# Right sums of layer 1 kept as single products in HBM, and a set order for squares, query copies, weight sums and gated sums

## The chip, the cores and the metric

The kernel runs on one core of one Trainium2 chip. The metric is the device time of one execution in microseconds (us); a kernel is compared by the median of several runs. A core has TensorE (PE, matmuls; PEld are its weight loads), VectorE (DVE), ScalarE (ACT), GpSimd (POOL) and SyncE (SP), each with its own queue of instructions that runs in order. Here SP issues the loads of weights, and POOL issues the small transfers between SBUF and HBM, among them those that add to what stands at their destination. One core needs no exchange with others.

## The reference

A trunk of two layers on 256 tokens of width 2048, in float32. Each layer has an attention part (four differential heads and eight latent heads, one output projection) and a dense MLP of width 8192 with a squared ReLU. Every part is modulated by a conditioning vector. Cut to what matters here:

```python
cond = jax.nn.silu(c)
for l in range(DEPTH):                                   # 2
    mod = cond @ w_ada[l] + b_ada[l]                     # 2048 x 12288
    sh_a, sc_a, g_a, sh_m, sc_m, g_m = split(mod, 6)
    h = _rmsnorm(x) * (1.0 + sc_a) + sh_a
    proj = h @ w_in[l]
    ...                                                  # out_a: differential, out_b: latent attention
    q  = _rmsnorm(cq, q_norm_g[l]) @ w_uq[l]
    kv = _rmsnorm(ckv, kv_norm_g[l]) @ w_ukv[l]
    mix = concatenate([out_a, out_b]) @ w_o[l]           # 2048 x 2048
    x = x + g_a * mix
    h = _rmsnorm(x) * (1.0 + sc_m) + sh_m
    y = square(relu(h @ w_mlp_in[l])) @ w_mlp_out[l]     # 2048 x 8192, 8192 x 2048
    x = x + g_m * y
return _rmsnorm(x, final_norm_g)
```

## The kernel before

**Tiles.** The 256 tokens are two groups t of 128, the 2048 columns of x four groups c of 512; x stays in SBUF. A float32 weight of 1 MB is loaded by SP into a tile `raw` (7 buffers) and split: ScalarE writes its high half `hi` (L158), VectorE the low half `lo` = raw - hi (L161), 4 buffers each. Activations are split likewise, and a product is three matmuls (high by high, low by high, high by low), summed in one of 8 PSUM banks. Intermediate tiles of 256 KB come from a pool of 40 called `u`.

**Order.** Each engine's order comes from the scheduler of the framework, which places instructions as they are written and by its own estimate of when their inputs are there. `behind(a, b)` adds that a stands behind b on their engine without waiting for it.

**Conditioning.** `cond @ w_ada` is done on VectorE: 192 transfers of 1 MB, and for each a multiply that also sums along the row (L387, tile `ada`). `more_ada` puts these sums behind the last `lo` of each weight group, and lets out new transfers at a rate that each stage sets (`RATE_...`): so many per weight group. Each gate or shift is needed at a fixed point later; `ada_need` does what is then still missing.

**w_o.** `rows` makes one column group c of a projection from four weight groups kq (L318, L319: high halves, then L321: low halves, 24 matmuls in each). Behind each c, `updates` lets VectorE multiply the two results by the gate (`yg`, L1425) and add them to x (L1427), and ScalarE square the new x and sum along the row (`sq`, L1441), which the next norm needs.

**Latent queries.** In the attention of layer 1, ScalarE copies query products out of PSUM (`qn`, L353) for the scores (`psm`, L1676), between copies of keys, softmax work and the high halves of `w_uv`.

**The MLP of layer 1** is four blocks fb of 2048 hidden columns. Where `block_by_seven` works, a 2 by 2 block product takes seven products and not eight: `mixed` adds quarters of the activation (`comb`, L1314 to L1317, split into `sh` and `sl`), `seven` adds quarters of the weights (`comb`, L1345 to L1347) and sums seven products over the block in seven banks. The loop over m in steps of 2 makes two columns of hidden tiles and the *left* products (columns 0 to 1023 of the output). At the end of a block `keep` copies each out of PSUM (`part`, L353) and POOL writes or adds it to a tile `kept` in HBM (L1262). The last block (fb = 3) reads the eight left tiles back (`acc`, L1114), combines them (`merged`) and multiplies them by the gate.

`right_by_seven` makes the *right* products (columns 1024 to 2047) of blocks 0 to 2. Its first half takes all eight products directly; its second half takes seven from the mixed halves of the hidden tiles. These were stored in HBM in the loop over m for the last four steps (`stored`, L1172) and are read back (`again`, L1181, tile `sr`), two steps ahead, by POOL. Then `keep_product` adds each of the eight to every output block that it belongs to, by the table `IN_BLOCKS`: 16 entries for four blocks (t, c), so products are added together by the transfers, 15 of them behind the loops. The last block makes its own right columns directly (`last_right`) and adds the four kept blocks to x by `add_rows`: a multiply by the gate on VectorE (L1119), then a transfer that adds to x.

The order around the change is thus set by POOL's single queue (stores, additions, reads in one order), by VectorE's queue, where sums of weights, low halves and combinations share one engine, and by ScalarE's, where high halves, copies and squares do.

Of the kernel before, what the change touches and what calls it, by code (L numbers as in the profile page):

```python
# [19 lines left out]
NK = D // P  # L20
# [49 lines left out]
def consts():  # L70
# [38 lines left out]
class Trunk:  # L109
# [43 lines left out]
    def part(self, raw, i, half, after=None, hi_after=None):  # L153

        v = raw[:, i * half : (i + 1) * half]
        hi = self.wp.tile([P, half], F32R, tag="hi", name=self.name("hi"), bufs=4)
        lo = self.wp.tile([P, half], F32R, tag="lo", name=self.name("lo"), bufs=4)
        ins = self.nc.scalar.activation(hi, v, AF.Copy)  # L158
        if hi_after is not None:
            self.behind(ins, hi_after)  # L160
        ins = self.nc.vector.tensor_tensor(lo, v, hi.bitcast(F32), ALU.subtract)  # L161
        if after is not None:
            self.behind(ins, after)
        return (hi, lo), ins
# [158 lines left out]
    def rows(self, src, xs, c, last=False):  # L323

        pss = [self.bank("pr") for _ in range(2)]
        for kq in range(2 if last else 4):
            if last and kq == 1:
                self.first_squares()
            self.rows_by_k(pss, self.weights(src[c, kq]), xs, kq)
        if last:  # L330
            self.quiet = True
            w = [self.weights(src[c, kq]) for kq in (2, 3)]
            for t in range(2):
                for kq in (2, 3):
                    self.rows_by_k(pss, w[kq - 2], xs, kq, (t,))
        return pss
# [14 lines left out]
    def copy(self, ps, name, scale=1.0):  # L351
        t = self.u(name)
        self.nc.scalar.activation(t, ps, AF.Copy, scale=scale)  # L353
        return t
# [63 lines left out]
    def setup(self):  # L418
        nc, io, cp = self.nc, self.io, self.cp
        self.ada_plan()  # L420
        self.cond = cp.tile([P, D], F32, name="cond")
# [467 lines left out]
    def layer(self, l, acc=None):  # L889
# [31 lines left out]
        q = []  # L921
# [21 lines left out]
        def up_q(b):  # L943
            qn.extend(self.copy(ps, "qn", ms) for ps in self.small(io["w_uq"][l, b], cq, 4))

# [106 lines left out]
        self.rate = RATE_K1 if l else RATE_K  # L1052
# [63 lines left out]
    def add_rows(self, y, t, c):  # L1116

        y = y.rearrange("p a b -> p (a b)")
        self.nc.vector.tensor_tensor(y, y, self.row[:, 512 * c : 512 * c + 512], ALU.mult)  # L1119
        self.nc.gpsimd.dma_start(self.xs_of(t, c), y, accum_op=ALU.add)  # L1120

    def block_by_seven(self, l, fb, h, banks):
# [4 lines left out]
        end = fb == NFB - 1  # L1127
        self.rate = RATE_S[l]
        for m in range(0, plain, 2):
            hid += self.relu2(self.joined(banks[m : m + 2], self.t("sum")))  # L1130
        for m in range(plain, NK, 2):
            both = self.t("sum")
            for j in range(2):
                src = io["w_m11"][NK * fb + m + j - 6] if l else io["w_m10"][NK * fb + m + j - 12]
                ps = self.wides([src], h)[0]
                self.join(ps, both[:, j])
                if len(pairs) > 1:
                    pairs[-2][j]()
            r = self.relu(both)
# [45 lines left out]
    def right_by_seven(self, fb, hid, plain, stored, light):  # L1185
# [20 lines left out]
        self.keep_product(8, begun[1][1])  # L1206
# [7 lines left out]
        for i in (1, 2, 3, 5, 7, 6, 4):  # L1214
            self.keep_product(i, sums[i - 1])

    def keep_product(self, i, ps):

        t = self.copy(ps, "part")
        for z in IN_BLOCKS[i]:  # L1220
            self.keep_tile(z, t)

    def last_right(self, hid, sums):
# [10 lines left out]
        def rows(c):  # L1234
            for t in range(2):
                self.add_rows(acc[t, c], t, c)

        light = [
            lambda: add(3, 5), lambda: add(7, 6, 4), lambda: rows(2),
            lambda: halves.extend(self.merged(acc)), lambda: rows(3),  # L1240
            lambda: done(halves[0], 0), lambda: done(halves[1], 1),
        ]
        self.read_kept(acc, list(range(1, 9)) + [(t, c) for c in (2, 3) for t in range(2)])
# [79 lines left out]
    def seven(self, src, parts, mixed, sums, first, last, begun=()):  # L1323
# [15 lines left out]
        def five():  # L1339
# [5 lines left out]
            add(comb[:, :1024], raw[:, 512:1536], raw[:, :1024], ALU.subtract)  # L1345
# [83 lines left out]
    def updates(self, pss, c, last=False):  # L1429

        for t in range(2):
            self.update(pss[t].rearrange("p a b -> p (a b)"), t, c)
            if last:
                self.squares(t, c)

# [363 lines left out]
```

## Time and profile before

| | us |
|---|---|
| median of 3 runs (range) | 2140.66 (2140.23 to 2140.73) |
| the profiled execution | 2141.52 |
| its span, first to last instruction | 2139.6 |
| TensorE busy | 2107.5 |
| VectorE busy | 1854.9 |
| ScalarE busy | 1287.6 |
| GpSimd busy | 136.1 |

All times in the trace are from the start of the span. w_o of layer 0 runs at about 300 to 395 us, the attention of layer 1 at 1100 to 1345, its MLP blocks 0 to 3 from about 1473, 1614, 1789 and 1959 on, each with its right products at the end. The granted clock of TensorE is 0.999 of full speed over the whole span. A line number such as L161 is a line of the kernel before; in the changed kernel the same code stands 3 lines earlier to 11 lines later.

### The profile page before, as it was taken

The page shows a single profiled execution, that of the slowest core. Times are in us where ns is not written, and L with a number is a line of the kernel's source. Part 1 is how long each engine was busy: PE and PEld are TensorE (multiplying, and loading weights), DVE is VectorE, ACT ScalarE, POOL GpSimd, SP SyncE. Part 2 cuts the span into 40 slices and gives each one's busy share as a digit, 9 for nine tenths or more (in the row PEclk, how much of TensorE's full clock was granted, in tenths as well). Part 3 has the DMA queues.
Part 4 walks back from the last instruction along what each step waited for, and adds up shares of the span by engine and source line. Part 5 has one row for each costly group of instructions (what it writes and reads, how often), then busy time and mean ns, then how long its engine had stood idle before and what let it go on. Part 6 is the DMA issues. An engine that isn't in the chain of part 4 may idle for free.

```text
span 2139.6 us, 30063 instructions
## 1 busy us (share of the span) xinstructions
PE 2107.5 (98%) x11327; PEld 1821.2 (85%) x11327; DVE 1854.9 (87%) x2515; ACT 1287.6 (60%) x1904; POOL 136.1 (6%) x202
## 2 busy tenths in 40 slices
PE   7999999999999999999999999999999999999998
PEld 6899888898888888888889998888888888888886
DVE  8889888989799888879978897889988997898898
ACT  6555663564466566646454576647667666676674
POOL 0000000000000100111000000000022022012110
PEclk9999999999999999999999999999999999999999
DMA  9999898789965965899978877877689699679864
GB/s 396 423 386 341 320 352 352 283 316 405 383 218 189 372 226 211 296 404 381 388 261 319 305 288 282 298 302 266 225 309 324 223 302 285 224 228 311 252 228 148
DMA packets 110674, 643.04 MB, mean 301 GB/s; under 512 B 12800, under 2 KB 13248, under 8 KB 43712
## 3 DMA queue, kind: packets, MB, share of 16 engines
q1 hardware_dynamic: 85536, 586.41, 72.0%
q0 software_dynamic: 24272, 53.52, 10.2%
q8 instruction: 88, 1.44, 0.3%
q10 hardware_dynamic: 720, 1.19, 0.2%
q14 instruction: 58, 0.48, 0.1%
HBM read 602.25 MB, written 35.68 MB: 298 GB/s over the span
## 4 chain that ended last, share of the span: by engine, by line
PE 89%; DVE 4%; DMA 4%; issue 2%; ACT 1%; POOL 0%; SPq 0%; ACTq 0%; DVEq 0%; POOLq 0%
PE ps L224 19%; PE ps L227 10%; PE pr L318 7%; PE pr L321 7%; PE pr L319 7%; PE pp L1336 3%; PE pp L1337 3%; PE pp L1335 3%; PE pk L267 3%; DMA ada<-in_w_ada 2%; PE pk L201 2%; PE pk L205 2%; PE pk L204 2%; DVE lo L161 2%; PE pk L291 2%
## 5 line engine op out<-in xcount | busy, mean ns | idle before, releaser
L158 ACT ACTIVATE hi<-raw 128x1024 fp32r<-128x1024 f32 (+2 forms) x714 | 707.1, 1003 | 469.5 <-PE pr L319 127.2
L161 DVE TENSOR_TENSOR lo<-raw,hi 128x1024 fp32r<-128x1024 f32 (+2 forms) x714 | 807.7, 1150 | 175.7 <-ACT hi L158 107.3
L387 DVE SCALAR_TENSOR_TENSOR ada<-ada,cond 128x2048 f32<-128x2048 f32 x192 | 438.3, 2285 | 13.8 <-DMA ada<-in_w_ada 12.8
L224 PE MATMUL ps<-h,hi 128*128 128x512 f32 x1856 | 442.1, 391 | 0.9 <-DVE sum L1504 0.4
L224 PEld LDWEIGHTS ps<-h,hi 128*128 128x128 f32 x1856 | 343.8, 188 | 77.5 <-DVE sum L1504 6.7
L227 PEld LDWEIGHTS ps<-h,lo 128*128 128x128 f32 x1856 | 236.4, 191 | 8.1
L227 PE MATMUL ps<-h,lo 128*128 128x256 f32 x1856 | 238.9, 283 | 0.0
L318 PE MATMUL pr<-hi,hidh 128*128 128x512 f32 x448 | 174.4, 389 | 0.1
L319 PE MATMUL pr<-hi,hidl 128*128 128x512 f32 x448 | 174.3, 389 | 0.0
L161 DVE TENSOR_TENSOR lo<-comb,hi 128x1024 fp32r<-128x1024 f32 x114 | 138.8, 1220 | 8.0 <-ACT hi L158 3.6
L158 ACT ACTIVATE hi<-comb 128x1024 fp32r<-128x1024 f32 x114 | 120.2, 1055 | 30.3 <-PE pp L1337 12.3
L321 PE MATMUL pr<-lo,hidh 128*128 128x512 f32 x448 | 111.4, 389 | 0.0
L318 PEld LDWEIGHTS pr<-hi,hidh 128*128 128x128 f32 x448 | 84.1, 188 | 18.0 <-ACT hi L158 0.5
L321 PEld LDWEIGHTS pr<-lo,hidh 128*128 128x128 f32 x448 | 84.0, 188 | 17.6 <-DVE lo L161 0.2
L319 PEld LDWEIGHTS pr<-hi,hidl 128*128 128x128 f32 x448 | 84.1, 188 | 17.4
L201 PE MATMUL pk<-h,hi 128*128 128x256 f32 x320 | 90.4, 285 | 0.2 <-ACT h L722 0.2
L205 PE MATMUL pk<-h,lo 128*128 128x256 f32 x320 | 90.5, 283 | 0.0
L204 PE MATMUL pk<-h,hi 128*128 128x256 f32 x320 | 90.5, 283 | 0.0
L1262 POOL DMA_DIRECT2D kept<-part x76 | 67.0, 989 | 332.0 <-ACT part L353 257.4
L1503 ACT ACTIVATE sum<-ps 128x256 f32<-128x256 f32 x110 | 41.8, 383 | 75.5 <-PE ps L227 74.3
L267 PE MATMUL pk<-hf,w 128*128 128x256 f32 x384 | 83.9, 379 | 0.0
L267 PEld LDWEIGHTS pk<-hf,w 128*128 128x128 f32 x384 | 72.6, 190 | 10.2 <-ACT hf L694 0.4
(307 smaller groups left out, 3844.3 us busy)
## 6 DMA issues: line engine op xcount, KB each, us to landing
ada<-in_w_ada SPq DMA_DIRECT2D x192, 1024.0 KB, 7.5
raw<-in_w_m SPq DMA_DIRECT2D x166, 1024.0 KB, 7.5
raw<-in_w_ms SPq DMA_DIRECT2D x48, 1024.0 KB, 6.2
raw<-in_w_o SPq DMA_DIRECT2D x32, 1024.0 KB, 7.1
kept<-part POOLq DMA_DIRECT2D x100, 256.0 KB, 9.2
raw<-in_w_mr SPq DMA_DIRECT2D x24, 1024.0 KB, 6.4
raw<-in_w_m SPq DMA_DIRECT2D x24, 768.0 KB, 5.8
raw<-in_w_dv SPq DMA_DIRECT2D x16, 1024.0 KB, 5.0
```

The source lines that it names most:

```text
L158: ins = self.nc.scalar.activation(hi, v, AF.Copy)
L161: ins = self.nc.vector.tensor_tensor(lo, v, hi.bitcast(F32), ALU.subtract)
L201: ins = mm(ps, hi, x[0], start=first, stop=False, skip_group_check=shared)
L204: mm(ps, hi, x[1], start=False, stop=False, skip_group_check=shared)
L205: self.last_mac = mm(ps, lo, x[0], start=False, stop=last, skip_group_check=shared)
L224: mm(ps.rearrange("p a b -> p (a b)"), part(w, k, 0), x[2], start=k == 0, stop=False)
L227: mm(ps[:, 0], part(w, k, 1), x[0], start=False, stop=k == nk - 1)
L267: self.nc.tensor.matmul(ps, v, whole[k], start=first, stop=last, skip_group_check=True)
L318: mm(ps, xh[:, c], part(i, 0), start=kq == 0 and i == 0, stop=False)
L319: mm(ps, xl[:, c], part(i, 0), start=False, stop=False)
L321: self.last_mm = mm(ps, xh[:, c], part(i, 1), start=False, stop=kq == 3 and i == 3)
L387: ins = nc.vector.scalar_tensor_tensor(w, w, 1.0, self.cond, ALU.mult, ALU.mult, accum_out=acc[:, i : i + 1])
```

## The change

- `updates` no longer squares a column group at once except the last; `late_squares` does it behind the making of the second weight group (kq = 1) of the next c. In the same place, `rows` makes the weights ahead of what follows.
- In layer 1 the high halves of `w_uv` are put behind the first query copies.
- The first of the weight combinations (`comb`) and the multiply of `add_rows` are put behind the latest `lo` on VectorE.
- The rate of transfers in the norm ahead of the MLP of layer 1 goes from 0.4 to 0, in that ahead of its attention from 0.4 to 0.3, in the blocks of layer 1 from 0.2 to 0.25 per weight group.
- Right products are kept once each under a key ("r", i): 8 stores per block. In the last block `right_steps` reads the eight at its start into `u` tiles, adds them to one another by eight transfers from SBUF to SBUF (`IN_ORDER`, one per product step), and calls `add_rows` for the four results in the last two steps of the loop over m.
- The mixed halves of the last m are used from SBUF; three pairs and not four are stored and read, and read one step earlier.
- The gate of the MLP of layer 1 is made ready in block 2 and not in block 3.

```diff
-RATE_A0, RATE_V, RATE_A1, RATE_A2, RATE_K, RATE_K1, RATE_M0 = 1.1, 1.6, 0.7, 1.0, 0.6, 0.4, 1.0
+RATE_A0, RATE_V, RATE_A1, RATE_A2, RATE_K, RATE_K1, RATE_M0 = 1.1, 1.6, 0.7, 1.0, 0.6, 0.3, 1.0
-RATE_S, RATE_R, RATE_E = (0.1, 0.2), (0.8, 0.2), 0.0
+RATE_S, RATE_R, RATE_E = (0.1, 0.25), (0.8, 0.2), 0.0
-IN_BLOCKS = {
-    1: ((0, 2), (0, 3), (1, 2), (1, 3)), 2: ((0, 2),), 3: ((0, 3),), 4: ((1, 2),),
-    5: ((0, 3), (1, 3)), 6: ((0, 3), (1, 2), (1, 3)), 7: ((1, 2), (1, 3)), 8: ((1, 3),),
-}
+IN_ORDER = ((6, 1), (2, 1), (7, 6), (4, 7), (6, 5), (3, 6), (5, 7), (5, 8))
...
         for kq in range(2 if last else 4):
+            w = self.weights(src[c, kq])
+            if kq == 1:
+                self.late_squares()
             if last and kq == 1:
                 self.first_squares()
-            self.rows_by_k(pss, self.weights(src[c, kq]), xs, kq)
+            self.rows_by_k(pss, w, xs, kq)
...
-            w = self.weights(io["w_uv"][l])
+            w = self.weights(io["w_uv"][l], order=(after_queries[0], None) if l else None)
...
-        self.rate = RATE_K1 if l else RATE_K
+        self.rate = 0.0 if l else RATE_K
...
-        self.nc.vector.tensor_tensor(y, y, self.row[:, 512 * c : 512 * c + 512], ALU.mult)
+        ins = self.nc.vector.tensor_tensor(y, y, self.row[:, 512 * c : 512 * c + 512], ALU.mult)
+        self.behind(ins, self.low)
...
+        right = self.right_steps() if l and end else []
...
+                if m and right and (len(right) > 4 or m >= NK - 4):
+                    right.pop(0)()
...
-                stored[m // 2] = self.stored(mixed)
+                stored[m // 2] = mixed if m == NK - 2 else self.stored(mixed)
...
-            if end and m == 2:
+            if l and fb == NFB - 2 and m == 2:
                 self.gate(l, 5)
...
+        mixed[2 * n - 1] = stored[2 * n - 1]
         for q in range(n):
-            if q > 1:
-                mixed[n + q - 2] = self.again(stored[n + q - 2])
+            if q:
+                mixed[n + q - 1] = self.again(stored[n + q - 1])
...
-            if q + 2 < 2 * n:
-                mixed[q + 2] = self.again(stored[q + 2])
...
         for i in (1, 2, 3, 5, 7, 6, 4):
-            self.keep_product(i, sums[i - 1])
+            self.keep(("r", i), sums[i - 1])
...
+    def right_steps(self):
+
+        acc = {}
+        self.read_kept(acc, [("r", i) for i in (1, 6, 2, 7, 4, 5, 3, 8)])
+        add = lambda i, j: self.nc.gpsimd.dma_start(acc["r", i], acc["r", j], accum_op=ALU.add)
+        out = {2: (0, 2), 4: (1, 2), 3: (0, 3), 5: (1, 3)}
+        return [lambda p=p: add(*p) for p in IN_ORDER] + [
+            lambda i=i, tc=tc: self.add_rows(acc["r", i], *tc) for i, tc in out.items()]
...
-        self.read_kept(acc, list(range(1, 9)) + [(t, c) for c in (2, 3) for t in range(2)])
+        self.read_kept(acc, range(1, 9))
...
-            add(comb[:, :1024], raw[:, 512:1536], raw[:, :1024], ALU.subtract)
+            self.behind(add(comb[:, :1024], raw[:, 512:1536], raw[:, :1024], ALU.subtract), self.low)
...
-            if last:
+            if last and c == 3:
                 self.squares(t, c)
+            elif last:
+                self.later.append((t, c))
```

Three places show how the order of the engines moves. The rows give line, operation, outputs and inputs with their numbers, and shape.

VectorE in w_o of layer 0, at the update of column group 1: before, then changed. `lo` are low halves of the next group's weights, `ada` a sum for the conditioning, `base` an addition of the squares.

```order
L161 TENSOR_TENSOR lo_3228<-raw_3221,hi_3227 128x1024
L1425 TENSOR_TENSOR yg_3209<-pr_3057,bias 128x512
L387 SCALAR_TENSOR_TENSOR ada_3183,macc_84<-ada_3183,cond 128x2048
L1427 TENSOR_TENSOR x<-x,yg_3209 128x512
L1425 TENSOR_TENSOR yg_3214<-pr_3058,bias 128x512
L1427 TENSOR_TENSOR x<-x,yg_3214 128x512
L1449 TENSOR_TENSOR base_3049<-xsq_3048 128x2
```
```order
L158 TENSOR_TENSOR lo_3224<-raw_3217,hi_3223 128x1024
L1428 TENSOR_TENSOR yg_3209<-pr_3051,bias 128x512
L1428 TENSOR_TENSOR yg_3212<-pr_3052,bias 128x512
L1430 TENSOR_TENSOR x<-x,yg_3209 128x512
L1430 TENSOR_TENSOR x<-x,yg_3212 128x512
L387 SCALAR_TENSOR_TENSOR ada_3183,macc_84<-ada_3183,cond 128x2048
L1460 TENSOR_TENSOR base_3105<-xsq_3104 128x2
```

The weight sum moves from between the first product and its addition to x to a place behind both additions. At column group 2 the two low halves that stood between products and additions move behind them in the same way. ScalarE's rows for this place (high halves and squares) are in the same order in both kernels.

ScalarE in the attention of layer 1, from the last softmax of the differential heads to the first of the latent heads (`sm`): before, then changed. `hi` from raw_11849 and raw_11931 (before), raw_11846 and raw_11927 (changed) are weights of the value and the next product.

```order
L1587 ACTIVATE s_11692,tot_11698<-s_11692,mx_11693 128x256 x2
L158 ACTIVATE hi_11855<-raw_11849 128x1024
L158 ACTIVATE hi_11933<-raw_11931 128x1024
L158 ACTIVATE hi_11937<-raw_11931 128x1024
L353 ACTIVATE qn_11749<-pss_11724 128x512
L353 ACTIVATE qn_11776<-pss_11751 128x512
L353 ACTIVATE aT_11783<-pt_11778 128x512
```
```order
L1598 ACTIVATE s_11689,tot_11695<-s_11689,mx_11690 128x256 x2
L353 ACTIVATE qn_11745<-pss_11720 128x512
L353 ACTIVATE qn_11772<-pss_11747 128x512
L353 ACTIVATE aT_11779<-pt_11774 128x512
L155 ACTIVATE hi_11848<-raw_11846 128x1024
L353 ACTIVATE aT_11826<-pt_11821 128x512
L155 ACTIVATE hi_11852<-raw_11846 128x1024
```

The two query copies now stand ahead of all these high halves.

GpSimd in the right products of block 1 of layer 1, from the first kept right products on: before, then changed.

```order
L1181 DMA sr_16362<-mixed_15829 128x512
L1181 DMA sr_16401<-mixed_15983 128x512
L1262 DMA kept_14778<-part_16398 128x512
L1181 DMA sr_16403<-mixed_15985 128x512
L1181 DMA sr_16452<-mixed_16139 128x512
L1181 DMA sr_16454<-mixed_16141 128x512
L1262 DMA kept_14966<-part_16585 128x512
L1262 DMA kept_14968<-part_16585 128x512
L1262 DMA kept_14970<-part_16585 128x512
```
```order
L1187 DMA sr_16303<-mixed_15811 128x512
L1187 DMA sr_16342<-mixed_15963 128x512
L1265 DMA kept_14595<-part_16339 128x512
L1187 DMA sr_16344<-mixed_15965 128x512
L1265 DMA kept_14768<-part_16382 128x512
L1265 DMA kept_14948<-part_16561 128x512
L1265 DMA kept_14952<-part_16564 128x512
L1265 DMA kept_14956<-part_16567 128x512
L1265 DMA kept_14960<-part_16570 128x512
```

Before, three reads of mixed halves stand behind the first store of a right product (part_16398); changed, the last read stands ahead of it (part_16382), and each product behind it is stored once.

More of the change, by code (lines that the diff above doesn't have):

```diff
@@ L160, in part @@
             self.behind(ins, hi_after)
-        ins = self.nc.vector.tensor_tensor(lo, v, hi.bitcast(F32), ALU.subtract)
+        ins = self.low = self.nc.vector.tensor_tensor(lo, v, hi.bitcast(F32), ALU.subtract)
         if after is not None:
@@ L420, in setup @@
         self.ada_plan()
+        self.later = []
         self.cond = cp.tile([P, D], F32, name="cond")
@@ L920, in layer @@
             ckr = self.joined(banks[4:], self.u("ckr"))
-        q = []
+        q, after_queries = [], []
         cq, ckv = [], []
@@ L1214, in right_by_seven @@
         for i in (1, 2, 3, 5, 7, 6, 4):
-            self.keep_product(i, sums[i - 1])
[L1217 to L1221, printed above, removed]
+            self.keep(("r", i), sums[i - 1])
[6 more added lines that the diff above has]
+            lambda i=i, tc=tc: self.add_rows(acc["r", i], *tc) for i, tc in out.items()]
     def last_right(self, hid, sums):
@@ L1232, in add @@
                 op(acc[i], sums[i - 1], acc[i], ALU.add)
-        def rows(c):
-            for t in range(2):
-                self.add_rows(acc[t, c], t, c)
         light = [
-            lambda: add(3, 5), lambda: add(7, 6, 4), lambda: rows(2),
-            lambda: halves.extend(self.merged(acc)), lambda: rows(3),
+            lambda: add(3, 5), lambda: add(7, 6, 4), lambda: halves.extend(self.merged(acc)),
             lambda: done(halves[0], 0), lambda: done(halves[1], 1),
         ]
-        self.read_kept(acc, list(range(1, 9)) + [(t, c) for c in (2, 3) for t in range(2)])
+        self.read_kept(acc, range(1, 9))
         add(1, 2)
@@ L1432, in updates, with late_squares @@
             self.update(pss[t].rearrange("p a b -> p (a b)"), t, c)
-            if last:
+            if last and c == 3:
                 self.squares(t, c)
+            elif last:
+                self.later.append((t, c))
+    def late_squares(self):
+        for t, c in self.later:
+            self.squares(t, c)
+        self.later = []
     def squares(self, t, c):
```

5 lines of the change are left out of this document (3 added, 2 removed).

## The prediction

> **What bounds the kernel now.** I read the page's busy shares first, then TensorE's waits by line, then, for each wait that the change touches, the chain or the timeline of the engine that ended it.
>
> ```profile
> span 2139.6 us, 30063 instructions
> ...
> PE 2107.5 (98%) x11327; PEld 1821.2 (85%) x11327; DVE 1854.9 (87%) x2515; ACT 1287.6 (60%) x1904; POOL 136.1 (6%) x202
> ```
>
> TensorE is the bound. Its order holds the same work before and after, so the change can only take from the 2139.6 - 2107.5 = 32.1 us in which it stands still, or add to them. The view of waits says where these lie; its columns are line, releaser, total, times, longest.
>
> ```profile
> PE pn L668 <- DVE rms L666: 5.1, 1, 5.1
> ...
> PE pr L1337 <- DMA sr<-mixed: 2.8, 3, 1.3
> ...
> PE pr L318 <- ACT hi L158: 1.9, 2, 1.0
> PE psm L1676 <- ACT qn L353: 1.3, 1, 1.3
> ...
> PE pk L291 <- DVE h L727: 1.0, 2, 0.5
> ...
> PE pp L1335 <- ACT hi L158: 0.9, 1, 0.9
> ...
> PE ps L224 <- DVE sum L1504: 0.4, 2, 0.2
> ```
>
> The longest, 5.1 us, is in the first norm, which the change leaves alone. The other six rows are what it touches: 2.8 + 1.9 + 1.3 + 1.0 + 0.9 + 0.4 = 8.3 us. That is little, and each piece has to be followed by itself.
>
> **The squares behind w_o of layer 0.** The chain there (start, us, what):
>
> ```profile
> 349.54 0.69 DVE yg L1425
> 350.23 2.21 DVE ada L387 x2
> 352.44 0.60 DVE x L1427
> 353.04 0.62 DVE yg L1425
> 353.68 0.70 DVE x L1427
> 355.13 0.95 ACT hi L158
> 356.13 0.50 PE pr L318
> 356.63 0.23 PE pr L319
> ...
> 376.85 0.61 DVE x L1427
> 378.12 1.05 ACT hi L158
> 379.21 0.50 PE pr L318
> ```
>
> ScalarE's high half of the second weight group stands behind two squares, these behind VectorE's x, and a 2.21 us weight sum stands between yg and x. In the changed order ScalarE's rows at this place read as before, the squares still ahead of the high half; what moved is on VectorE, where both yg and both x now stand together and the sum behind them. So the high half starts some 2.2 us earlier at the first place. At the second the two low halves (1.22 us each, quoted below for another place) go behind x, and x is done 2.3 us earlier. Both are more than the 1.0 us wait, so 1.9 us go. Against that, the low halves of the first weight group come 1.2 us later at two places. TensorE needs them 16 matmuls of 0.23 us, 3.7 us, after the group begins; yg, yg, x, x and one low half take 0.61 + 0.61 + 0.60 + 0.60 + 1.22 = 3.6 us. That is level, and I charge 0.5 us. Net: 1.4 us.
>
> **The pairs of mixed halves that come back.** GpSimd's timeline, then the landing times of tile sr:
>
> ```profile
> 1758.82 0.53 POOL L1181 DMA_DIRECT2D sr<-mixed  x1 [1.05 <-PE pr L1304]
> 1768.75 0.89 POOL L1262 DMA_DIRECT2D kept<-part  x1 [9.41 <-ACT part L353]
> 1769.32 1.95 POOL L1181 DMA_DIRECT2D sr<-mixed  x3
> ```
> ```profile
> DMA to landing us min/median/max: 5.3/10.0/15.5
> ```
>
> Three of the eight reads stand behind a store that waits 9.41 us for ScalarE, start at 1769.3 and land up to 15.5 us later, when TensorE already waits. In the changed order there are three pairs instead of four, and all six reads stand ahead of that store; the fourth pair stays in SBUF. The last read then goes out at about 1759 and lands by 1774.5 even with 15.5 us; TensorE's first wait of this kind ends at 1779.6. All 2.8 us go, with 5 us to spare.
>
> **The query copies of layer 1.** ScalarE's timeline:
>
> ```profile
> 1267.34 1.99 ACT L158 ACTIVATE hi<-raw 128x1024 fp32r<-128x1024 f32 x2
> 1270.21 1.06 ACT L158 ACTIVATE hi<-raw 128x1024 fp32r<-128x1024 f32 x1 [0.88 <-PE pv L305]
> 1271.18 1.07 ACT L353 ACTIVATE qn<-pss 128x512 f32<-128x512 f32 x2
> ```
>
> The first qn stands behind a high half that waits 0.88 us for TensorE to free its slot, while TensorE waits for qn. The new order has both qn ahead of these high halves: 1.3 us go. The high and low halves of w_uv come about 1.1 us (two qn) later in exchange, and the pv products need them; I charge 0.3. Net 1.0.
>
> **The norm of layer 1.** VectorE's, then TensorE's timeline:
>
> ```profile
> 1127.07 2.28 DVE L387 SCALAR_TENSOR_TENSOR ada<-ada,cond 128x2048 f32<-128x2048 f32 x1
> ```
> ```profile
> 1131.47 1.67 PE L291 MATMUL pk<-h,hi 128*128 128x512 f32 x6 [0.53 <-DVE h L727]
> ```
>
> Of three sums in this norm only the third moves, behind the norm's last low half. Its wait of 0.53 us goes, the other half of the 1.0 us stays.
>
> **The second block of layer 1.** Here the 0.9 and 0.4 us lie, 1.3 together. VectorE's timeline and the window:
>
> ```profile
> 1657.93 1.23 DVE L1345 TENSOR_TENSOR comb<-raw 128x1024 f32<-128x1024 f32 x1 [0.80 <-DMA raw<-in_w_ms]
> ```
> ```profile
> 1700.00:1750.00 50.00, 48.98 (x246) 40.92 (x245) 47.53 (x64) 36.57 (x49) 8.93 (x14) 1.00 0.80 273
> ```
>
> VectorE is busy 47.53 of 50 us where the 0.9 us lie. The comb additions now go behind the latest low half, so one that waits for its weights no longer stands ahead of a ready low half, and 8 stores of products per block take the place of 15. But the block gets a fourth sum of 2.28 us. I take half: 0.7 us.
>
> **Starting again.** The chain above shows 0.50 us for the matmul after a wait, 0.23 for its neighbour: 0.27 us per wait that goes, beside the idle time. Two squares, three sr, qn, the norm and half of three others are 8.5 waits: 2.3 us.
>
> Gains together: 1.4 + 2.8 + 1.0 + 0.5 + 0.7 + 2.3 = 8.7 us.
>
> **What is new.** Two sums move into the start of the third block, and four row products (add_rows, in before L1119) with their additions go into steps 12 and 14 of the last block. Rows: VectorE's timeline at two steps of the third block, the window of the last block, and tile acc.
>
> ```profile
> 1857.16 1.83 DVE L161 TENSOR_TENSOR lo<-raw,hi 128x1024 fp32r<-128x1024 f32 x2 [2.04 <-PE ps L227]
> ...
> 1861.10 1.22 DVE L161 TENSOR_TENSOR lo<-raw,hi 128x1024 fp32r<-128x1024 f32 x1
> ...
> 1873.45 1.83 DVE L161 TENSOR_TENSOR lo<-raw,hi 128x1024 fp32r<-128x1024 f32 x2 [2.39 <-PE ps L227]
> ```
> ```profile
> 2030.00:2060.00 30.00, 30.00 (x163) 25.92 (x162) 27.77 (x39) 21.46 (x27) 0.00 (x0) 1.00 0.59 204
> ```
> ```profile
> L1119 DVE TENSOR_TENSOR acc<-acc,bias x12: 681/684/686, 988.9 to 2104.3; 128x512 f32<-128x512 f32 x12
> ...
> DMA to landing us min/median/max: 2.9/10.2/20.4
> ```
>
> A step of the third block leaves VectorE 2.0 to 2.4 us, a sum takes 2.28: level. The last block leaves 30 - 27.77 = 2.23 us where four products of 0.68 ask for 2.7. If all of it is uncovered it costs 2 x 2.28 + 2.7 = 7.3 us; if the idle time takes it, nothing. The rows are nearer to covered, so I take a third, 2.5 us. The four products that leave the end of the last block free VectorE there, where TensorE has no wait, so that is worth nothing. The moved gate and its DMAs stand on a GpSimd queue with room at both places (busy 6% on the page): nothing either.
>
> Net: 8.7 - 2.5 = 6.2 us. The profiled execution took 2141.52 us, so 2135.3 by its measure; the runs' median, 2140.66, is 0.86 below it, so the forecast is **2134.5 us**.
>
> **The rivals.** *Nothing hides what is new*: all 7.3 us of VectorE's new work push TensorE. For it: 87% busy, and 47.53 of 50 in one stretch. Against it: the 2 us of idle time in each step quoted. Then 8.7 - 7.3 = 1.4 us remain: 2139.3.
>
> *More than counted*: all 8.3 us but the norm's 0.5 go, ten restarts give 2.7, and the new work hides: 7.8 + 2.7 = 10.5, so 2130.2. For it: the idle time in the steps. Against it: reordered engines nearly always leave a new wait of some tenths.
>
> *The squares don't move*: ScalarE's order is unchanged there, and if the high half in truth waits for its weights, 1.4 + 0.5 us fall away: 2136.4. Against it: the chain there goes from x by way of ScalarE to the high half, and over no transfer.
>
> *Slower: the sums in the last block come late.* The right products are now read into eight SBUF tiles and added by accumulating DMAs, each of which needs the one before. GpSimd's timeline and its DMA issues show how stores that follow one another go in before, VectorE's timeline one place in the last block:
>
> ```profile
> 1976.48 0.86 POOL L1262 DMA_DIRECT2D kept<-part  x1 [3.07 <-DMA kept<-part]
> ```
> ```profile
> kept<-part POOLq DMA_DIRECT2D x100, 256.0 KB, 9.2
> ```
> ```profile
> 2045.59 1.21 DVE L1345 TENSOR_TENSOR comb<-raw 128x1024 f32<-128x1024 f32 x1
> ```
>
> Before, the last stores of this kind were still going out at 1976 and after; with half of them I estimate that they end near 1972 and, with the slowest read quoted, 20.4, that the reads are in by 1995. The second product stands three rows ahead of the comb addition that ran at 2045.59, so VectorE reaches it at about 2041; three additions in a row stand ahead of it. The last two products stand ahead of the next comb addition, some 8 to 12 us on, at 2053 to 2057, and five additions ahead of them. At 9.2 us each the fifth ends at 2041, in time. The point from which it decides is (2053 - 1995) / 5 = 11.6 us. At 15.5 us, the longest quoted for this size on this queue bar one, it ends at 2072, 19 us late; VectorE stands, with all its low halves behind it, and TensorE has some 4 us of ready weights: 15 us lost against 6.2 won, 2149.5. Against it: DMA engines are only 0.59 busy in that window, and 9.2 us holds for busier stretches. The Trainium skill, page "DMA: Bandwidth & Descriptors", section "Rules for kernel authors", says that an accumulating DMA beside another access of the same bytes must wait for the earlier one's semaphore, since nothing holds the bytes between its read and its write. By that rule the five can't overlap; the wait of 3.07 us in the row above agrees, and no run yet shows an addition between two tiles in SBUF.
>
> **How the numbers follow.** A measurement of this kernel tells 0.2%, 4.3 us, from no change: faster is below 2136.4, slower above 2144.9. Forecast 0.47 (2131 to 2138; 0.40 faster, 0.07 same). Nothing hides 0.25 (0.04, 0.17, 0.04 slower). More than counted 0.14, all faster. Squares stay 0.06 (half faster, half same). Late sums 0.08 (0.01 same, 0.07 slower). Together 0.61 faster, 0.28 same, 0.11 slower. The range runs from 2129.5, just under the larger gain, to 2141.5, just over the case that hides nothing; about 0.04 lie below and 0.16 above.
>
> **What would show it.** In the waits after: no row of L1337 for sr, none of psm for qn, none of L318 for hi, one and not two of pk for h. In the timeline of the last block: VectorE's four row products without a wait for acc. A wait of ps for a sum or of a product for a low half in the first steps of the third block, or steps 12 and 14 of the last, would show the new work uncovered; a wait for acc above 3 us on VectorE would make the forecast wrong.

## The result

The change makes the kernel slower: 2174.07 us in the median of five runs (2171.45 to 2176.30), against 2140.73 for the kernel before beside it (2140.23 to 2143.94). The ratio is 1.0152, with a 95% interval of 1.0137 to 1.0167. The forecast was 2134.5 us.

The page of the changed kernel, in the lines that answer to those of before, and then the line of the page before that gives the shares of the chain:

```profile
span 2169.5 us, 29993 instructions
...
PE 2119.8 (98%) x11327; PEld 1820.8 (84%) x11327; DVE 1854.3 (85%) x2515; ACT 1289.4 (59%) x1904; POOL 119.1 (5%) x181
...
PE 86%; DVE 10%; ACT 2%; DMA 1%; issue 1%; SPq 0%; DVEq 0%; ACTq 0%
```
```profile
PE 89%; DVE 4%; DMA 4%; issue 2%; ACT 1%; POOL 0%; SPq 0%; ACTq 0%; DVEq 0%; POOLq 0%
```

The work is what it was: the same 11327 matmuls, VectorE busy 1854.3 us against 1854.9, ScalarE 1289.4 against 1287.6. TensorE's busy time is 12.3 us longer (2119.8 against 2107.5), most of it because a matmul beside a wait counts longer than one in a row of them (0.39 us and more, where the next one usually starts after 0.23). The granted clock is not the cause: it is 0.996 here and 0.999 before, and 0.996 too in the run e1_comb_free, which has no loss. What grew is VectorE's share of the chain that ended last, from 4% to 10%. TensorE's waits, in the view that gives line, releaser, total, times and longest:

```profile
PE pp L1339 <- DVE lo L158: 9.5, 12, 1.6
PE ps L221 <- DVE sum L1515: 6.7, 23, 0.4
...
PE pp L1338 <- ACT sh L1322: 3.3, 2, 2.0
...
PE pr L1339 <- DVE lo L158: 2.6, 6, 0.4
PE pp L1338 <- ACT hi L155: 1.7, 3, 0.6
...
PE pk L288 <- DVE h L728: 0.4, 1, 0.4
```

The rows that were to go are gone: none for sr, none for qn (psm), none for the high half behind the squares, one and not two for h of the norm. In their place stand waits in the blocks, 23 of them for a `sum`, where the kernel before had 2.

Where in the program the time went is seen by setting the starts of equal matmuls side by side (both kernels have 11327). The table is worked out from the two traces (that of the changed kernel is of its fastest run, 2171.45 us); it gives the start in the kernel before and how much later the same matmul of the changed kernel starts.

```
matmul  place                               before, us   changed: later by, us
 1800   w_o of layer 0                         330.8         +0.6
 2100   behind it                              398.4         -1.1
 3300   layer 0, block 1 begins                597.7         -1.2
 4800   layer 0, block 2, right                891.5         +4.9
 5700   end of layer 0                        1068.3         +8.0
 6300   layer 1, behind the norm              1171.3         +7.3
 7200   layer 1, behind the query copies      1303.3         +6.3
 8100   layer 1, block 0                      1485.8         +6.3
 9600   layer 1, block 2 begins               1790.4        +17.6
10500   layer 1, block 3                      1968.2        +25.0
11326   last matmul                           2130.8        +29.5
```

Where squares, norm and query copies stand, the changed kernel gains: 1.8 us at the squares, 0.7 at the norm, and 1.0 net up to the query copies. In every block by seven products, two of layer 0 and four of layer 1, it loses. The right products, the moved sums and the gate are edits to layer 1; in the blocks of layer 0 only the places of the weight combinations (`comb`) and of the gated products (`add_rows`) differ.

What a step of such a block loses shows on VectorE. Its timeline in block 2 of layer 1, of the kernel before and then of the changed one:

```profile
1857.16 1.83 DVE L161 TENSOR_TENSOR lo<-raw,hi 128x1024 fp32r<-128x1024 f32 x2 [2.04 <-PE ps L227]
1858.91 0.42 DVE L1504 SCALAR_TENSOR_TENSOR sum<-ps,sum 128x256 f32<-128x256 f32 x1
1859.24 1.22 DVE L1345 TENSOR_TENSOR comb<-raw 128x1024 f32<-128x1024 f32 x1
```
```profile
1875.87 1.23 DVE L158 TENSOR_TENSOR lo<-raw,hi 128x1024 fp32r<-128x1024 f32 x1 [2.04 <-PE ps L224]
1877.01 1.22 DVE L1348 TENSOR_TENSOR comb<-raw 128x1024 f32<-128x1024 f32 x1
1878.15 0.42 DVE L1515 SCALAR_TENSOR_TENSOR sum<-ps,sum 128x256 f32<-128x256 f32 x1
```

And TensorE's timeline at that moment, changed kernel:

```profile
1877.94 0.39 PE L1338 MATMUL pp<-hi,hidh 128*128 128x512 f32 x1
1878.62 3.70 PE L221 MATMUL ps<-h,hi 128*128 128x512 f32 x15 [0.28 <-DVE sum L1515]
```

`sum` takes a result out of PSUM and so frees the bank for the next one. It used to come ahead of the combination; now the combination stands between low half and `sum`, and `sum` ends at 1878.57 (1878.15 + 0.42). The matmul that waits for it starts 0.68 us after the one ahead of it, where 0.23 is usual: 0.45 us lost, of which the row shows 0.28, since the end of a matmul is put at 0.39 us behind its start. 23 such places make 10.3 us.

At the last step of a block and in the right products the loss has another form. The last step of block 2 of layer 1, in the timelines of ScalarE, VectorE and TensorE:

```profile
1927.65 1.06 ACT L155 ACTIVATE hi<-comb 128x1024 fp32r<-128x1024 f32 x1 [1.05 <-PE pp L1340]
```
```profile
1928.75 1.23 DVE L158 TENSOR_TENSOR lo<-comb,hi 128x1024 fp32r<-128x1024 f32 x1 [0.72 <-ACT hi L155]
1929.89 1.22 DVE L1348 TENSOR_TENSOR comb<-raw 128x1024 f32<-128x1024 f32 x1
```
```profile
1934.38 0.50 PE L1339 MATMUL pp<-lo,hidh 128*128 128x512 f32 x1 [1.60 <-DVE lo L158]
```

ScalarE's high half of a combination waits for TensorE, VectorE's low half waits for that high half, the next combination stands behind this low half, and TensorE then waits 1.60 us for a low half of the weights of that combination's group. The changed kernel's chain in the right products of block 2 of layer 1 (start, us, what):

```profile
1967.33 1.07 ACT hi L155
1968.40 0.02 issue
1968.43 1.22 DVE lo L158
1969.65 1.14 DVE comb L1348
1970.79 0.60 DVE lo L158
1971.39 0.60 DVE comb L1349
1971.99 1.14 DVE lo L158
1973.13 0.61 DVE comb L1350
...
1973.85 1.07 ACT hi L155
1974.91 0.02 issue
1974.94 1.23 DVE lo L158
1976.16 1.14 DVE comb L1348
```

No TensorE stands in it: the high half of one combination (ScalarE), its low half, then the next combination, then again a high half, 6.5 us for a turn. The latest low half at the time when `comb` is written is here the one of the combination before. So each combination now waits for ScalarE's high half of the last one, and VectorE can no longer run ahead.

Counted from start to start like the 10.3 us, TensorE's waits at the last steps of the six blocks come to 11.8 us (1.76 us in four of them, 2.7 and 2.0 in the other two), and those in the right products of three blocks to 9.1 us.

### The profile page after: what moved, and what is told of

It reads as the page before. It is cut to its first block, busy times and chain, and to the rows that moved or that the text cites. A ratio compares the mean times of both kernels' runs of the same rounds, so it can differ in the third digit from the quotient of the medians.

```text
span 2169.5 us, 29993 instructions
## 1 busy us (share of the span) xinstructions
PE 2119.8 (98%) x11327; PEld 1820.8 (84%) x11327; DVE 1854.3 (85%) x2515; ACT 1289.4 (59%) x1904; POOL 119.1 (5%) x181
## 4 chain that ended last, share of the span: by engine, by line
PE 86%; DVE 10%; ACT 2%; DMA 1%; issue 1%; SPq 0%; DVEq 0%; ACTq 0%
PE ps L221 19%; PE ps L224 9%; PE pr L318 7%; PE pr L315 7%; PE pr L316 7%; DVE lo L158 4%; PE pk L264 3%; PE pp L1339 2%; PE pp L1340 2%; DVE comb L1348 2%; PE pk L198 2%; PE pp L1338 2%; PE pk L202 2%; PE pk L201 2%; PE pk L288 2%; PE pv L302 2%
## 5 line engine op out<-in xcount | busy, mean ns | idle before, releaser
L1339 PE MATMUL pp<-lo,sh 128*128 128x512 f32 x189 | 74.6, 394 | 2.3 <-DVE lo L158 2.3
```

## Experiments

Theory A: the place of the combination behind the latest low half makes the loss. Theory B: the right products make it, by their reads and their additions between tiles in SBUF. Theory C: the moved sums of weights do.

### The combination put back, and alone

```diff
-            self.behind(add(comb[:, :1024], raw[:, 512:1536], raw[:, :1024], ALU.subtract), self.low)
+            add(comb[:, :1024], raw[:, 512:1536], raw[:, :1024], ALU.subtract)
```

in the changed kernel, all else left:

> The changed kernel with one edit undone: the first weight combination is no longer put behind the latest low half on VectorE. Theory A (that place makes VectorE and ScalarE wait for one another by turns, and in the profile of the changed kernel the waits of TensorE for a sum, a low half or a combination that came with it add up to about 33 us): 2141 us, within 4. Theory B (the loss comes from the right products, their reads and their additions in the last block): the loss stays, 2168 us or more. Theory C (it comes from the moved sums of weights in the blocks): 2168 or more too.

Measured: 2143.34 us against 2142.45 for the kernel before beside it, ratio 1.0004 (0.9995 to 1.0014), inside what theory A said. The loss is gone, and so is any gain.

The opposite, this one edit in the kernel before:

> The kernel before with this one edit alone: the first weight combination behind the latest low half. Theory A: nearly the whole loss appears, 2172 us, within 6, with TensorE waiting 0.45 us for a sum in most steps of the blocks. Theories B and C: no loss to speak of, 2139 to 2143.

Measured: 2176.23 us, ratio 1.0155 (1.0140 to 1.0170), again inside what theory A said. Its waits:

```profile
PE pp L1336 <- DVE lo L161: 10.7, 12, 1.6
PE ps L224 <- DVE sum L1504: 6.6, 23, 0.4
```

The same two rows as in the changed kernel. Theory A holds in both directions: with this edit 33.8 us over the kernel before, without it 0.9. Theories B and C do not explain this loss.

### How the edit costs it

Two runs take the edit in pieces. In the first, the combination goes behind the low half of a whole weight group (a left operand of the hidden product), never behind the low half of another combination; `self.low` is set in `weights` and no longer in `part`:

```diff
-        ins = self.low = self.nc.vector.tensor_tensor(lo, v, hi.bitcast(F32), ALU.subtract)
+        ins = self.nc.vector.tensor_tensor(lo, v, hi.bitcast(F32), ALU.subtract)
...
+        self.low = ins
         self.more_ada(ins)
```

> The changed kernel, with the weight combination put behind the latest low half of a whole weight group only, no longer behind the low half of the combination before it. Theory A1 (the loss comes from pinning a combination to the low half of the one before, which waits for ScalarE, which waits for TensorE): the waits in the right products and at the last step of each block go, some 20 us, and what stays is the wait of 0.45 us for a sum in each step, since the combination still stands ahead of that sum: 2152 us, within 5. Theory A2 (any pin costs it all): 2170 or more.

In the second it is put there in the loops over the steps and left free in the right products:

```diff
-            self.behind(add(comb[:, :1024], ...), self.low)
+            ins = add(comb[:, :1024], ...)
+            if not begun:
+                self.behind(ins, self.low)
```

> The changed kernel with the weight combination put behind the latest low half in the loops over the steps of a block alone, and free in the right products. By the trace of the changed kernel the right products of three blocks hold five waits of about 0.7 us each, some 10 us, and the loops the rest, 0.45 us in each of 22 steps and 1.8 us at the last step of each of six blocks: 2164 us, within 4. If the loss of the right products is not of that edit: 2174.

Measured: 2163.74 us, ratio 1.0104 (1.0088 to 1.0121), and 2163.10 us, 1.0101 (1.0087 to 1.0115). The second was met: of the changed kernel's loss some 10 us lie in the right products (its last matmul is 29.5 us late, that of this run 19.9; by the medians, 33.3 and 20.4 us over the kernel before, it is 13) and the rest in the loops. The first came out 12 us above what theory A1 said, and 6 below theory A2. Waits of the two, in this order:

```profile
PE ps L222 <- DVE sum L1516: 6.6, 23, 0.4
...
PE pp L1340 <- DVE lo L159: 5.0, 11, 0.6
```
```profile
PE pp L1339 <- DVE lo L158: 7.8, 8, 1.6
PE ps L221 <- DVE sum L1517: 6.6, 23, 0.4
```

The 23 waits for `sum` are the same in both, so either pin in the loop brings them. The wait at the last step of four of the six blocks is 1.76 us with a pin to any low half and 0.74 us with a pin to weight groups, measured from start to start, so the pin to the combination before is worth about 1 us there. Both pieces of the theory are seen, but A1 had laid too much on the pin to the combination before: it takes 11 us of the loss (33.3 us over the kernel before with it, 22.2 without), not some 20. In the first run TensorE loses 0.6 to 1.1 us at about ten further places of layer 1, and what orders these was not taken apart.

### The gated products, and the right products alone

The changed kernel with this undone too, in `add_rows`:

```diff
-        self.behind(ins, self.low)
```

> The changed kernel with two edits undone: neither the weight combination nor the multiply of the gated sums is put behind the latest low half. In the changed kernel TensorE waits 1.1 us for a low half and stands about 3 us longer in the last block of layer 0, beside the four gated products. If these are put there by the second edit: 3 us below the run with one edit undone, 2138 us. If not: the same as that run within 1 us.

and the kernel before with the right products alone as in the changed kernel (kept once, three stored pairs, read and added in the last block, gate in block 2), without any pin:

> The kernel before with the right products alone as in the changed kernel: each kept once, three stored pairs and not four, the eight read and added in the last block, the gate a block earlier. Theory A: the waits for mixed halves go and nothing comes in their place, 2137.5 us, within 2. Theory B: 2155 us or more, with VectorE or GpSimd waiting in the last block for additions between two tiles in SBUF.

Measured: 2167.96 us, ratio 1.0115 (1.0098 to 1.0132), and 2169.14 us, 1.0123 (1.0108 to 1.0138). The first expectation failed by 30 us: freeing the gated products does not win 3 us, it costs 25. In the second, theory A failed by 32 us, and theory B's time came, with its sign. VectorE in the last block of the second of these kernels, then TensorE:

```profile
1991.12 0.69 DVE L1116 TENSOR_TENSOR acc<-acc,bias 128x512 f32<-128x512 f32 x1 [17.74 <-DMA acc<-acc]
...
2007.98 0.69 DVE L1116 TENSOR_TENSOR acc<-acc,bias 128x512 f32<-128x512 f32 x1 [7.03 <-DMA acc<-acc]
...
2013.04 0.69 DVE L1116 TENSOR_TENSOR acc<-acc,bias 128x512 f32<-128x512 f32 x1 [3.76 <-DMA acc<-acc]
```
```profile
1993.73 2.08 PE L224 MATMUL ps<-h,lo 128*128 128x256 f32 x8 [7.75 <-DVE lo L158]
...
2015.65 0.79 PE L1333 MATMUL pp<-lo,sh 128*128 128x512 f32 x1 [12.92 <-DVE lo L158]
```

GpSimd's timeline there shows that each addition is issued only when the one that it builds on has landed:

```profile
1990.21 0.85 POOL L1220 DMA_DIRECT2D acc<-acc  x1 [4.93 <-DMA acc<-acc]
...
2009.76 0.87 POOL L1220 DMA_DIRECT2D acc<-acc  x1 [6.61 <-DMA acc<-acc]
```

This is the wait that the prediction had in its slower rival, though here the products are early and not the sums late. Nothing held the products where they are written, in the last two steps, and the scheduler put the first near the start of the block, where VectorE reached it at 1973.4 us (1972.96 + 0.41), before GpSimd had issued more than one of the eight reads. VectorE stood 28.5 us in three waits with its low halves behind it, and TensorE ran dry. Pinned behind the low half of their step, as in the changed kernel, the products run at 2080 to 2101 us (2050 to 2070 in e1_comb_free) and wait for nothing. So the second pin of the change is needed for the third part of it, and theory B is true of a kernel without that pin, not of the changed kernel. The two losses have different causes, a misplaced pin and a missing one, and no run here has both.

### Where the gains went

With the combination free the changed kernel keeps its gain up to block 1 of layer 1 and then gives it back. Starts of equal matmuls against the kernel before, worked out from the traces (us, negative is earlier):

```
matmul  place                            e1_comb_free  e8_no_right  e6_rows_early  e11_one_back_rates
 1800   w_o of layer 0                       +0.6         +0.9          +1.2           +0.6
 2100   behind it                            -1.2         -1.0          -0.6           -1.2
 6300   layer 1, behind the norm             -2.2         -1.9          -1.7           -1.4
 7200   behind the query copies              -3.2         -3.0          -2.7           -2.9
 9300   layer 1, block 1, step 12            -4.6         -3.1          -4.3           -1.9
 9600   layer 1, block 2 begins              -2.8         -1.1          -2.4           -3.1
10500   layer 1, block 3                     -3.3         -1.4          -0.4           -2.3
11326   last matmul                          -0.1         -1.4          -0.6           -2.4
```

Two places give it back in e1_comb_free: 1.8 us around 1740 us, and 3.2 us at the end. Three runs were made for them first.

Sums of weights in the blocks at the old rate (`RATE_S` of layer 1 back from 0.25 to 0.2):

> The changed kernel without the edit on the weight combinations (as in e1_comb_free), and the rate of weight sums in the blocks of layer 1 back at 0.2. In e1_comb_free VectorE runs without a pause from 1718 to 1742 us with the fourth sum in it, and TensorE then waits 1.4 and 0.9 us. If the fourth sum does that: about 2.5 us below e1_comb_free there; over the whole run 1 to 2.5 us less, since a sum more comes at the start of the third block. If the waits come from the order of the products alone: the same as e1_comb_free within 1 us.

The four gated products one turn of the loop over m earlier (`m >= NK - 6` in place of `NK - 4`):

> As e1_comb_free, with the four gated products in steps 10 and 12 of the last block and not in 12 and 14. In e1_comb_free the reads of the left sums stand behind the four transfers that add these products to x, start at 2071 us rather than 2061, VectorE waits 4.6 us for them, and TensorE 3.2 us more at the end. If that is the cause: 3 us below e1_comb_free, with the first reads at 2061 or earlier and no wait of VectorE for them. If VectorE is merely full at the end: the same as e1_comb_free. If the additions between tiles in SBUF are not done by step 10 (they end near 2020, VectorE is there at about 2030): VectorE waits for them and it gets slower.

The right products, the gate's place and the combination (without a pin) as in the kernel before, all else changed:

> The kernel before with all edits but two: the right products as before, and the weight combination not put behind a low half. That leaves the squares, the query copies, the moved sums and the gated products. By e1_comb_free's trace these save 3.2 us up to the MLP of layer 1 and about 1.4 in its second block, and the waits for mixed halves stay: 2137 us, within 2. If the right products alone were what e1_comb_free loses again behind that point, this run is 3 us or more below it; if the sums are, it is not.

Measured: 2141.04 us, ratio 0.9996 (0.9986 to 1.0005); 2141.95 us, 1.0003 (0.9994 to 1.0013); 2140.97 us, 0.9995 (0.9986 to 1.0004). None differs from the kernel before, and none from e1_comb_free by more than the runs tell. So the 3 us expected of e6_rows_early and the 2137 us of e8_no_right did not come, and for e5_fewer_sums the runs do not decide between its two cases.

The traces say more than the times. In e1_comb_free GpSimd reads the left sums behind the four transfers that wait for the gated products, and VectorE waits for these reads. Its timeline of GpSimd, then VectorE:

```profile
2070.72 0.87 POOL L1123 DMA_DIRECT2D x<-acc  x1 [3.74 <-DVE acc L1121]
2071.26 4.13 POOL L1116 DMA_DIRECT2D acc<-kept  x7
```
```profile
2090.94 0.69 DVE L1240 TENSOR_TENSOR acc<-pp,acc 128x512 f32<-128x512 f32 x1 [3.32 <-DMA acc<-kept]
```

In e6_rows_early these reads go out from 2061.06 on, as in the kernel before, VectorE has no wait for them, and the last block loses nothing, where e1_comb_free loses 3.2 us (table). That part of the expectation holds. But the run is no faster, since VectorE's order in the right products of block 2 moved as well; there the fourth combination in a row waits for its weights, with low halves behind it:

```profile
1938.82 1.23 DVE L1348 TENSOR_TENSOR comb<-raw 128x1024 f32<-128x1024 f32 x1 [1.20 <-DMA raw<-in_w_mr]
```

TensorE then waits 2.25 us from start to start, where e1_comb_free has 1.04. This is just what the pin on the combination was there to prevent, and it needs a looser one. e5_fewer_sums likewise loses its waits at 1738 us and has three of about 1 us elsewhere, and 3.4 us at 1941. In e8_no_right two of the three waits for mixed halves go without the new right products: the two of 1.3 us. TensorE waits 0.7 and 0.4 us for low halves in their place, and the third, of 0.2 us, stays. Which of its edits moved them was not taken apart.

### A looser pin, and a version to keep

In the right products alone, the combination behind the last low half of the group before last, added to e6_rows_early:

```diff
-            add(comb[:, :1024], ...)
+            ins = add(comb[:, :1024], ...)
+            if begun and len(self.ends) > 1:
+                self.behind(ins, self.ends[-2])
...
+            w, ins = self.part(st["comb"], 1, 1024)
+            self.ends.append(ins)
```

> As e6_rows_early, and in the right products alone the weight combination is put behind the last low half of the group before last, so that VectorE can run one group ahead and not three. In e6_rows_early three combinations stand ahead of ready low halves at 1926 to 1940 us, the fourth waits 1.2 us for its weights, and TensorE then 2.2 us. If that order is the cause: these 2.2 us go and 2139 us come out, 2.5 below e6_rows_early. If the weights are simply late: the same as e6_rows_early.

The same with `RATE_S` at 0.2:

> As e9_pin_one_back, with the rate of weight sums in the blocks of layer 1 back at 0.2. In e6_rows_early TensorE waits 1.5 and 1.1 us at 1738 and 1740, behind the fourth sum of the second block; in e5_fewer_sums these waits are not there, but three of about 1 us at 1529, 1596 and 1653 are. If the fourth sum is worth its waits: about 1 us below e9_pin_one_back; if one order only takes the place of another: the same within 1 us.

and with all rates as in the kernel before:

> As e9_pin_one_back, with all rates of weight sums as in the kernel before. By the theory that the moved sums save 0.5 to 1 us in the norms and cost some 2 in the blocks: 1 us below e9_pin_one_back, 2138 us. If they save what was meant: 1 us above it.

Measured: 2142.41 us, ratio 1.0000 (0.9990 to 1.0009); 2141.07 us, 0.9992 (0.9983 to 1.0001); 2139.42 us, 0.9991 (0.9982 to 1.0000), each over eleven runs, beside 2142.72 us for the kernel before. The 2139 us expected of the first did not come; the second and third come out below it, as expected, but the intervals overlap. The wait at 1942 us is gone in e9_pin_one_back, which was the point of the pin, but waits of 0.7 and 0.4 us for low halves now stand in the right products of three blocks, where e6_rows_early has them in one, and the waits at 1740 us stay. The last version is the best of all: 2.4 us earlier at the last matmul in its trace, 0.09% in its runs, with an interval that ends at no change. It is not shown to beat the kernel before.

## Why the prediction was wrong

- **The second block of layer 1, 0.7 us of gain.** This is the step that failed. It said of the combinations that "one that waits for its weights no longer stands ahead of a ready low half" and took that for a gain of half of 1.3 us. The same edit measured alone costs 33.8 us. Three things were left out: that the edit acts in six blocks, two of layer 0 and four of layer 1; that with the pin the combination comes ahead of `sum`, which frees the bank (10.3 us); and that at the last steps and in the right products the latest low half is that of the combination before, which waits for ScalarE (at the last steps 11.8 us in all, in the right products 9.1, of which the pin to the combination before takes about 11; what orders the rest stays open). The sign named for uncovered new work, waits of ps for a sum, did come, but from the pin: e2_comb_only has none of the new work and the same 23. The prediction asked what stands behind the waiting combination and not what the combination itself now waits for. The changed order on VectorE (low half, combination, `sum`) could have been read from its rows beforehand; the three places set out ahead of the prediction are others.
- **The squares, 1.4 us and a restart for each of two waits.** Right: 1.8 us in e1_comb_free (from +0.6 to -1.2), by the cause named, VectorE's order and not ScalarE's.
- **The query copies, 1.0 us and one restart.** Right: 1.5 us, where the list had a wait of 1.3; the restart is there.
- **The norm, 0.5 us and one restart.** Right in size, 0.8 us; 0.5 us of it was given back right behind it.
- **Mixed halves, 2.8 us and three restarts.** The waits went, as forecast, but not all the time: waits for low halves took their place (in e1_comb_free 0.7 us and 0.4 us in the right products of block 1, 1.0 us in those of block 2). And e8_no_right loses the two long ones without that edit.
- **What is new, 2.5 us.** Too small, and at other places. What the term names cost nothing in e1_comb_free: it loses nothing over block 2 (from -2.8 to -3.3), and the four products wait for nothing. But it gave back 1.8 us around the fourth sum of block 1, which the prediction had set against that block's gain, and 3.2 us at the end. The second was not in the list: the row products' transfers stand ahead of the left reads on GpSimd, and of that queue the prediction looked at the moved gate alone. Without the combination's pin the forecast's 6.2 us would have come out as 0, near the time of the case in which nothing hides what is new (1.4 us of gain) but not by its mechanism.
- **The slower rival, late sums.** Its wait is real, at 25 us in the two kernels without the pin on the gated products, and absent where they are pinned, as the prediction's place for them (2041 to 2057 us) assumed. The link was 7.1 us (below), under the 11.6 from which it was to decide. The rival's sentence that no run yet shows an addition between two tiles in SBUF was wrong: the transfers that add to x, which stays in SBUF, are such additions, and the kernel before has twelve (last section).

## What to carry to other kernels

An instruction pinned behind another on an in-order engine waits for all that the other waits for, so ask of every pin what its anchor depends on: if the anchor is the previous link of the same loop by way of a second engine, the engine has lost its lookahead. A pin that helps at one place acts wherever the line is used, here in six blocks rather than the one with the waits, so count the uses, and look at which instruction ends up between a producer and the one that frees a PSUM bank. And where TensorE is busy 98%, removing single waits of 1 to 3 us can just move them: the gains at the squares, the norm and the query copies held (3.2 us), but e5_fewer_sums, e6_rows_early and e9_pin_one_back each lost a named wait and got others of 0.4 to 3.4 us elsewhere.

## What was not expected of the hardware

Additions between two tiles in SBUF by DMA, 256 KB each, landed 7.1 us after issue in the median of the changed kernel; transfers of that size to HBM, first writes and additions together, took 9.5:

```profile
kept<-part POOLq DMA_DIRECT2D x79, 256.0 KB, 9.5
...
acc<-acc POOLq DMA_DIRECT2D x8, 256.0 KB, 7.1
```

In the kernel with the right products alone they took 6.1 us. The additions to x in the kernel before, also from SBUF to SBUF, took less still, and the prediction had this row at hand when it priced the link at 9.2 us by the transfers to HBM:

```profile
x<-acc POOLq DMA_DIRECT2D x12, 256.0 KB, 4.7
```

A short wait of TensorE is shown about 0.17 us smaller than it is (0.28 us for 0.45), which in 23 places is nearly 4 us that the list of waits doesn't hold (10.3 against 6.7).
